# Down products of an FFN in pairs from block 0 on with a last group of four, and raw weights in twelve places of 2 KB

## The chip, the cores and the metric

The kernel runs on one core of a Trainium2 chip. The metric is the device time of one execution in microseconds, here the median of three runs. The engines are named as the profile names them: PE (TensorE matmul), PEld (its weight load), DVE (VectorE), ACT (ScalarE), POOL (GpSimd) and SP (SyncE, which issues every DMA of this kernel).

## What is computed

The input is 512 tokens `x` and 256 context tokens `ctx` of width 1024. The first block has two layers. Each layer is a half FFN, a mixer and a second half FFN, and each of them has its own norm, shift, scale and gate, all from one conditioning product (`ada_w`). In the last layer's second half the context is no longer needed. The second block is a gated delta rule branch and a dilated window attention branch. Cut to what matters here:

```
def swiglu(x, w_gu, w_down):
    gt, up = jnp.split(x @ w_gu, 2, axis=-1)
    return (jax.nn.silu(gt) * up) @ w_down

def half_ffn(h, g, shift, scale, gate, w_gu, w_down):
    return h + 0.5 * gate * swiglu(norm_mod(h, g, shift, scale), w_gu, w_down)

def first_block(...):
    for li in range(2):
        m = jnp.split((silu(c) @ ada_w[li] + ada_b[li]), 9)       # and mc from c_ctx
        h = half_ffn(h, norm_g[li, 0], m[0], m[1], m[2], ffn_w_gu[li, 0], ffn_w_down[li, 0])
        z = norm_mod(h, norm_g[li, 1], m[3], m[4])
        h = h + m[5] * mixer(z, zc)
        h = half_ffn(h, norm_g[li, 2], m[6], m[7], m[8], ffn_w_gu[li, 1], ffn_w_down[li, 1])
        # the same for the context hc, up to the second layer's mixer
```

`w_gu` is 1024 x 5632 and `w_down` 2816 x 1024, all in float32. There are four FFNs.

## The kernel before

**Number format.** Every float32 operand of a large product is split into a high part (`hi`, rounded for PE by an ACT copy) and the rest (`lo`, a DVE subtraction): `split`, `halves`. A product is then three matmuls, hi·hi, hi·lo, lo·hi (`mm3`).

**Raw weights.** `raw` (line 737) loads a piece of a weight matrix by a DMA on SP into a place of the tag `raw`. There are `RAW` = 5 places of 128 x 1024 float32, 4 KB on each partition, 512 KB in all. `split` makes `whi` and `wlo` of it, 512 columns at a time, in `PARTS` = 10 places each. A place is free again once the last reader of all of its 4 KB is done. The gates (`load_gate`, line 866), rows of 1024 values broadcast to all partitions, take places of the same tag, and hold them as long as they are needed.

**The FFN** (`ffn`, line 1071). The 2816 hidden features are 22 blocks of 128. For each block `gate_up` (line 1017) loads the two 1024 x 128 weight blocks and makes seven combinations of their quarters, `swiglu` runs seven products on half of the tokens each (banks named `gu`), and writes the activations `ah` and `al`, three places each. The down products (`down(g)`, line 1083) run over groups of blocks: for each tile of 128 tokens and each half of 512 columns, the blocks of the group are summed in one PSUM bank (`dn`), and the bank is then taken into the running sum `h`. The first group's bank is copied by ACT, that of later groups added by DVE, that of the last but one is added, multiplied by the gate and added to the residual `hin`, and that of the last is multiplied by the gate and added, after which the tile goes to `on_tile`: its norm, its transposes and what the next stage needs of it. Line 1078 sets the groups:

```
groups = [[0]] + [[f, f + 1] for f in range(1, NF - 4, 2)] + [list(range(NF - 3, NF))]
```

These are block 0 alone, nine pairs, and blocks 19 to 21. A group's down products are issued one block late, after `swiglu` of the block that follows the group's last one. In the loop over blocks `filler(f)` puts in conditioning units: `ada` (line 817) runs one 1024 x 512 part of `ada_w` in two halves of four matmuls that work side by side, and later fills the `mods` and gates.

The first three FFNs run on six tiles (768 tokens, `gu` matmuls of 384 columns), the last on four (256 columns). The stages are: FFN 1 (to about 595 us), the even mixer with its output product (to about 905 us), FFN 2 (to about 1460 us), FFN 3 (to about 1995 us), the odd mixer (to about 2265 us), FFN 4 (to about 2640 us), the second block.

**What sets the order.** The code above doesn't issue instructions; it records them (`Engine`, `Program.record`). `Program.order` (line 505) then plays a list scheduler with a cost for each instruction, counts the places of each tag, takes for each engine the earliest recorded instruction that can start, may move some between DVE, ACT and POOL (`others`), and `emit` writes the result in that order (line 693, which is why all instructions have that line). Each engine runs its list in order. So a change in places or groups moves instructions elsewhere too. An FFN's phase has `SCR` = 8 scratch places of 2 KB.

Of the kernel before, what the change touches and what calls it, by code (L numbers as in the profile page):

```python
# [10 lines left out]
F32 = mybir.dt.float32  # L11
F32R = mybir.dt.float32r
# [8 lines left out]
D = 1024  # L21
# [298 lines left out]
        ("gpsimd", "gpsimd"): 0.1}  # L320

KEEP = 1
RAW, PARTS = 5, 10
SCR = 8
CPLAN = "1567234"
XN = "vv"
PARK = "vavavava"
# [372 lines left out]
class Net:  # L700
# [34 lines left out]
        return self.t2(name).rearrange("p (a b) -> p a b", a=4)  # L735

    def raw(self, src, a, b):
        v = self.wp.tile([128, 1024], F32, tag="raw", name="raw", bufs=RAW)[:, :a * b].rearrange("p (a b) -> p a b", a=a)
        self.nc.sync.dma_start(v, src)
        return v  # L740

# [28 lines left out]

    def w_cols(self, w, c0, ncol, nk=KD, pool=None):
        ws = []
        kk = 1024 // ncol
        for k0 in range(0, nk, kk):
            ws += self.split(self.raw(w[k0 * 128:(k0 + kk) * 128, c0:c0 + ncol].rearrange("(k p) c -> p k c", p=128),
                                      kk, ncol), pool=pool if k0 < 4 else None)
        return ws

    def w_feats(self, w, c0):
        ws = [], []  # L780
        for k0 in (0, 512):
            r = self.raw(w[k0:k0 + 512, c0:c0 + 256].rearrange("(k p) c -> p k c", p=128), 4, 256)
            for i in range(2):
                ws[i].extend(self.split(r[:, :, i * 128:(i + 1) * 128]))
        return ws

    def proj_t(self, cols, ws):
# [29 lines left out]
    def ada(self, li, n):  # L817
        self.ada_end()


        nc, T = self.nc, self.T
        S = self.bank("ada")
        for k0 in (0, 4):
            r = [self.raw(T["ada_w"][li][k * 128:(k + 2) * 128, n * 512:(n + 1) * 512]
                          .rearrange("(k p) c -> p k c", p=128), 2, 512) for k in (k0, k0 + 2)]
            with nc.together(4):
                for k in range(k0, k0 + 4):
                    c = 32 * (k % 4)
                    nc.tensor.matmul(S[c:c + 32, :], self.scp[:, k, :], r[k % 4 // 2][:, k % 2, :],
                                     start=(k < 4), stop=(k >= 4), tile_position=(0, c))  # L830
        Ss = self.t2("adaSs")
        nc.vector.tensor_copy(Ss, S)
        self.open_ada.append((li, n, Ss))
# [32 lines left out]
    def load_gate(self, li, gi, nx=2):  # L866
        g = []
        for x in range(nx):
            t = self.wp.tile([128, D], F32, tag="raw", name=f"gate{x}", bufs=RAW)
            self.nc.sync.dma_start(t, self.gated[li, gi][x:x + 1, :].to_broadcast([128, D]))  # L870
            g.append(t)
        return g

    def rstd(self, ss, n, scale, eps):
# [142 lines left out]
    def gate_up(self, li, which, f):  # L1017

        nc = self.nc
        src = self.T["ffn_gu"][2 * li + which][f]  # L1020
        r = [self.raw(src[:, k:k + 4, :], 4, 256) for k in (0, 4)]
        a11, a12 = (x[:, :, 0:128] for x in r)
        a21, a22 = (x[:, :, 128:256] for x in r)
        s1, s2 = self.t24("ws"), self.t24("ws")
        sub = lambda d, x, y: nc.vector.tensor_tensor(d, x, y, op=OP.subtract)
        ws = {1: self.split(a11)}
        nc.gpsimd.tensor_tensor(s1, a21, a22, op=OP.add)
        sub(s2, s1, a11)
        ws[6] = self.split(s2)
        ws[5] = self.split(s1)  # L1030
        sub(a21, a11, a21)
        ws[7] = self.split(a21)
        ws[2] = self.split(a12)
        sub(a12, a12, s2)
        ws[3] = self.split(a12)
        ws[4] = self.split(a22)
        return ws
# [33 lines left out]
    def ffn(self, li, which, nt, F, hsrc, filler, on_tile, first=None):  # L1071
# [3 lines left out]
        ntok = nt * 128  # L1075
        n = ntok // 2
        z = self.operands(F.zx, n)
        groups = [[0]] + [[f, f + 1] for f in range(1, NF - 4, 2)] + [list(range(NF - 3, NF))]
        ends = [g[-1] for g in groups]
        acts = {}  # L1080
        gates = []
# [1 line left out]
        def down(g):  # L1083
            ws = {}
            for f in g:
                r = self.raw(wd[f * 128:(f + 1) * 128, :].rearrange("p (a b) -> p a b", a=2), 2, 512)
                ws[f] = self.split(r)
            left = len(groups) - 1 - groups.index(g)
            if left == 1:
                gates.extend(self.load_gate(li, 2 * which, 2 if nt > 4 else 1))  # L1090
            for t in range(nt):
                cs = at(t, nt)
                for half in range(2):
                    hs = slice(half * 512, (half + 1) * 512)
                    if left == 1:
                        x = self.t2("hin")
                        nc.sync.dma_start(x, hsrc(t)[:, hs])
                    ps = self.bank("dn")
                    self.mm3(ps, [(tuple(a[:, cs] for a in acts[f]), ws[f][half]) for f in g])
                    y = F.h[t][:, hs]  # L1100
                    if left == 0:
                        if HADD[t + 6 - nt] == "g":
                            tmp = self.t2("dtmp")
                            nc.vector.tensor_mul(tmp, ps, gates[0 if t < 4 else 1][:, hs])
                            nc.gpsimd.tensor_add(y, y, tmp)
                        else:
                            nc.vector.tensor_mul(ps, ps, gates[0 if t < 4 else 1][:, hs])
                            nc.vector.tensor_add(y, y, ps)
                    elif g[0] == 0:
                        nc.scalar.copy(y, ps)  # L1110
                    else:
                        nc.vector.tensor_add(y, y, ps)
                    if left == 1:
                        nc.vector.tensor_mul(y, y, gates[0 if t < 4 else 1][:, hs])
                        nc.gpsimd.tensor_add(y, y, x)
                if left == 0:
                    on_tile(t)

        F.new_h(nt)
        for f in range(NF):  # L1120
            ws = first if first and f == 0 else self.gate_up(li, which, f)
            acts[f] = tuple(F.ap.tile([128, ntok], F32R, tag=x, name=x, bufs=3) for x in ("ah", "al"))
            self.swiglu(ws, z, n, *acts[f], *([ORD0, "15"] if first and f == 0 else []))
            self.late = []
            filler(f)
# [6 lines left out]
    def out_proj(self, w, tiles0, hsrc, h, gates, on_tile):  # L1132
# [4 lines left out]
        for half, tiles in ((0, tiles0), (1, range(len(h)))):  # L1137
            hs = slice(half * 512, (half + 1) * 512)
            ws = self.w_cols(w, half * 512, 512)
            for t in tiles:  # L1140
                ps = self.proj_t(at(t, len(h)), ws)
                tmp = self.t2("otmp")
                nc.vector.tensor_mul(tmp, ps, gates[0 if t < 4 else 1][:, hs])
                (nc.vector if OADD[half] == "v" else nc.gpsimd).tensor_add(h[t][:, hs], h[t][:, hs], tmp)
                if half == 1:
                    on_tile(t)
# [408 lines left out]
    def dn_head(self, h, M, C, Pm, st, ones):  # L1555
# [16 lines left out]

        ws = []
        for c in (h, 4 + h, 8 + h, 12 + h):
            ws.append(self.split(self.raw(w_in[:, c * 128:(c + 1) * 128].rearrange("(k p) c -> p k c", p=128), KD, 128)))
        feats = []
        for i in range(4):
            ps = self.bank("dnp")
# [490 lines left out]
def layout(inputs):  # L2069
    a = {k: np.asarray(v) for k, v in inputs.items()}  # L2070
    arrays = {n: np.ascontiguousarray(a[n]) for n in _INS}
    arrays["ffn_gu"] = np.ascontiguousarray(
        a["ffn_w_gu"].reshape(4, KD, 128, 2, NF, 128).transpose(0, 4, 2, 1, 3, 5)).reshape(4, NF, 128, KD, 256)
    w = a["ev_w_out"][0]
    arrays["ev_w_out"] = np.concatenate([w[:512].reshape(2, 4, 64, D).transpose(1, 0, 2, 3).reshape(512, D), w[512:]])
    rpb = np.pad(a["d_rpb"][0], ((0, 0), (0, 0), (16, 16)))
# [24 lines left out]
```

## Time and profile before

| | |
|---|---|
| median of three runs | 3287.4 us (3286.73 to 3289.97) |
| profiled execution, device time | 3290.94 us |
| its span | 3289.0 us |
| PE busy | 3205.9 us (97%), 18198 matmul records |
| DVE busy | 2348.6 us (71%) |
| ACT busy | 1347.3 us (41%) |
| POOL busy | 263.2 us (8%) |
| DMA | 337.70 MB, mean 103 GB/s |
| mean granted clock of PE | 0.991 |

The span is the time from the first to the last profiled instruction; the device time of the same execution has 1.94 us around it. A float32 matmul that isn't split (`ada`, the transposes aside) shows as two records. Busy time of PE counts time under a lower granted clock as busy, so a loss can sit in the clock column of a stretch that looks full.

### The profile page before, as it was taken

How to read it: one execution, taken by the hardware profiler on the slowest of the kernel's cores; microseconds unless marked ns; L12 is line 12 of the kernel's file. 1: busy time of each engine (PE TensorE's matmuls, PEld its weight loads, DVE VectorE, ACT ScalarE, POOL GpSimd, SP SyncE). 2: the span in 40 equal slices, each digit the busy share in tenths (PEclk: the TensorE clock that was granted, in tenths of full speed). 3: DMA queues.
4: the chain of work that ended last, by engine and by line, in shares of the span. 5: the costliest groups of instructions: out<-in, count | busy, mean ns of one | idle time of the engine just before them, and what ended most of it. 6: DMA issues, size and time to landing. Idle time of an engine off the chain costs nothing.

```text
span 3289.0 us, 47391 instructions
## 1 busy us (share of the span) xinstructions
PE 3205.9 (97%) x18198; PEld 2796.0 (85%) x18198; DVE 2348.6 (71%) x4531; ACT 1347.3 (41%) x2773; POOL 263.2 (8%) x276
## 2 busy tenths in 40 slices
PE   7999999999999999989999999999999999999999
PEld 4889998776778999969999988867999888898987
DVE  7677768777677767797767786677888977667343
ACT  5333333644453333354333335445444444444331
POOL 0000001212100000010000002110000112231000
PEclk9999999999999999999999999999999999999999
DMA  7342123222444221252221233253322341121221
GB/s 258 119 158 78 65 70 122 94 78 90 154 163 148 77 74 62 91 188 85 77 77 58 72 121 102 83 176 124 113 99 97 123 144 46 39 77 61 90 90 64
DMA packets 161522, 337.70 MB, mean 103 GB/s; under 512 B 12256, under 2 KB 57696, under 8 KB 161168
## 3 DMA queue, kind: packets, MB, share of 16 engines
q1 hardware_dynamic: 161296, 334.68, 30.6%
q8 instruction: 143, 2.34, 0.3%
q14 instruction: 83, 0.68, 0.1%
HBM read 316.76 MB, written 17.87 MB: 102 GB/s over the span
## 4 chain that ended last, share of the span: by engine, by line
PE 86%; DVE 9%; DMA 2%; ACT 2%; issue 1%; POOL 0%; SPq 0%; ACTq 0%; DVEq 0%; POOLq 0%
PE gu L693 34%; PE dn L693 18%; PE pj L693 14%; PE pjf L693 5%; DVE h L693 2%; PE dnp L693 2%; PE ada L693 2%; PE sc L693 1%; PE tr L693 1%; PE fin L693 1%; PE yb L693 1%; PE dmm L693 1%; PE pv L693 1%; PE ptr L693 1%; DMA raw<-in_ffn_gu 1%
## 5 line engine op out<-in xcount | busy, mean ns | idle before, releaser
L693 ACT CAST whi<-raw 128x512 fp32r<-128x512 f32 x885 | 522.7, 620 | 665.7 <-PE gu L693 198.5
L693 DVE TENSOR_TENSOR wlo<-raw,whi 128x512 fp32r<-128x512 f32 (+1 forms) x846 | 560.7, 688 | 233.6 <-ACT whi L693 216.8
L693 DVE TENSOR_TENSOR gu<-gu 128x384 f32<-128x384 f32 (+1 forms) x616 | 319.5, 519 | 273.8 <-PE gu L693 260.8
L693 DVE TENSOR_TENSOR h<-h,dn 128x512 f32<-128x512 f32 x404 | 273.3, 681 | 67.3 <-PE dn L693 67.0
L693 PE MATMUL dn<-wlo,ah 128*128 128x512 f32 x968 | 310.9, 395 | 0.0
L693 PE MATMUL dn<-whi,ah 128*128 128x512 f32 x968 | 307.5, 396 | 0.0
L693 PE MATMUL dn<-whi,al 128*128 128x512 f32 x968 | 305.6, 395 | 0.0
L693 PE MATMUL gu<-zh,whi 128*128 128x384 f32 (+1 forms) x1408 | 287.9, 326 | 13.2 <-ACT zh L693 4.6
L693 PE MATMUL gu<-zh,wlo 128*128 128x384 f32 (+1 forms) x1408 | 288.5, 323 | 0.0
L693 PE MATMUL gu<-zl,whi 128*128 128x384 f32 (+1 forms) x1408 | 283.3, 322 | 0.2 <-DVE zl L693 0.2
L693 PEld LDWEIGHTS gu<-zh,whi 128*128 128x128 f32 x1408 | 237.4, 189 | 33.8 <-ACT zh L693 8.4
L693 PEld LDWEIGHTS gu<-zl,whi 128*128 128x128 f32 x1408 | 235.6, 189 | 3.8 <-DVE zl L693 2.4
L693 PEld LDWEIGHTS gu<-zh,wlo 128*128 128x128 f32 x1408 | 237.4, 190 | 0.0
L693 PE MATMUL gu<-zxh,wlo 128*128 128x384 f32 (+1 forms) x1056 | 219.1, 326 | 8.1 <-DVE wlo L693 8.1
L693 PE MATMUL gu<-zxh,whi 128*128 128x384 f32 (+1 forms) x1056 | 214.5, 328 | 1.9 <-ACT zxh L693 1.0
L693 PEld LDWEIGHTS dn<-wlo,ah 128*128 128x128 f32 x968 | 182.1, 188 | 40.0
L693 ACT CAST whi<-ws 128x512 fp32r<-128x512 f32 x176 | 105.8, 620 | 268.6 <-PE dn L693 212.6
L693 PEld LDWEIGHTS dn<-whi,al 128*128 128x128 f32 x968 | 181.8, 188 | 38.5 <-DVE al L693 0.2
L693 PE MATMUL gu<-zxl,whi 128*128 128x384 f32 (+1 forms) x1056 | 214.2, 325 | 0.0
L693 PEld LDWEIGHTS dn<-whi,ah 128*128 128x128 f32 x968 | 180.0, 189 | 37.5 <-ACT ah L693 1.9
L693 PE MATMUL pj<-whi,zh 128*128 128x512 f32 (+1 forms) x848 | 199.2, 369 | 6.1 <-ACT swP L693 3.1
L693 PEld LDWEIGHTS gu<-zxh,whi 128*128 128x128 f32 x1056 | 180.0, 190 | 21.3 <-issue 3.4
(391 smaller groups left out, 5225.8 us busy)
## 6 DMA issues: line engine op xcount, KB each, us to landing
raw<-in_ffn_gu SPq DMA_DIRECT2D x176, 512.0 KB
raw<-in_ada_w SPq DMA_DIRECT2D x144, 512.0 KB
raw<-in_ffn_w_down SPq DMA_DIRECT2D x88, 512.0 KB
raw<-in_w_in SPq DMA_DIRECT2D x72, 512.0 KB
raw<-in_od_w_in SPq DMA_DIRECT2D x16, 512.0 KB
raw<-in_ev_w_in SPq DMA_DIRECT2D x14, 512.0 KB
gate<-gate SPq DMA_DIRECT2D x10, 512.0 KB
raw<-in_ev_w_out SPq DMA_DIRECT2D x8, 512.0 KB
```

The costliest lines, as they stand in the source:

```text
L693: getattr(self.real[o.eng], o.fn)(*[real(x) for x in o.args], **{k: real(v) for k, v in o.kw.items()})
```

## The change

The first group is blocks 0 and 1, followed by eight more pairs, and the last group is blocks 18 to 21; the last but one group's gate and residual work so follows block 18 instead of 19. Activations have four places instead of three. A raw place is 2 KB and there are twelve: every load is at most 512 float32 on each partition, and the host lays `ffn_gu` out so that each quarter of a block's weights is one contiguous load. A gate is two loads. An FFN's phase has nine scratch places, and the program's scratch for dynamic DMAs is set to 1024 bytes.

```
-RAW, PARTS = 5, 10
-SCR = 8
+RAW, PARTS = 12, 10
+SCR = 9
...
     def raw(self, src, a, b):
-        v = self.wp.tile([128, 1024], F32, tag="raw", name="raw", bufs=RAW)[:, :a * b].rearrange("p (a b) -> p a b", a=a)
+        v = self.wp.tile([128, 512], F32, tag="raw", name="raw", bufs=RAW)[:, :a * b].rearrange("p (a b) -> p a b", a=a)
...
     def w_cols(self, w, c0, ncol, nk=KD, pool=None):
-        kk = 1024 // ncol
+        kk = 512 // ncol
...
     def w_feats(self, w, c0):
-            r = self.raw(w[k0:k0 + 512, c0:c0 + 256].rearrange("(k p) c -> p k c", p=128), 4, 256)
             for i in range(2):
-                ws[i].extend(self.split(r[:, :, i * 128:(i + 1) * 128]))
+                c = c0 + 128 * i
+                ws[i].extend(self.split(self.raw(w[k0:k0 + 512, c:c + 128].rearrange("(k p) c -> p k c", p=128), 4, 128)))
...
     def ada(self, li, n):
-            r = [self.raw(T["ada_w"][li][k * 128:(k + 2) * 128, n * 512:(n + 1) * 512]
-                          .rearrange("(k p) c -> p k c", p=128), 2, 512) for k in (k0, k0 + 2)]
+            r = [self.raw(T["ada_w"][li][k * 128:(k + 1) * 128, n * 512:(n + 1) * 512].unsqueeze(1), 1, 512)
+                 for k in range(k0, k0 + 4)]
...
     def load_gate(self, li, gi, nx=2):
-            t = self.wp.tile([128, D], F32, tag="raw", name=f"gate{x}", bufs=RAW)
-            self.nc.sync.dma_start(t, self.gated[li, gi][x:x + 1, :].to_broadcast([128, D]))
-            g.append(t)
+            g.append([self.wp.tile([128, 512], F32, tag="raw", name=f"gate{x}", bufs=RAW) for _ in range(2)])
+            for i, t in enumerate(g[x]):
+                self.nc.sync.dma_start(t, self.gated[li, gi][x:x + 1, i * 512:(i + 1) * 512].to_broadcast([128, 512]))
...
     def gate_up(self, li, which, f):
-        r = [self.raw(src[:, k:k + 4, :], 4, 256) for k in (0, 4)]
-        a11, a12 = (x[:, :, 0:128] for x in r)
-        a21, a22 = (x[:, :, 128:256] for x in r)
+        a11, a21, a12, a22 = (self.raw(src[:, i], 4, 128) for i in range(4))
...
     def ffn(self, li, which, nt, F, hsrc, filler, on_tile, first=None):
-        groups = [[0]] + [[f, f + 1] for f in range(1, NF - 4, 2)] + [list(range(NF - 3, NF))]
+        groups = [[f, f + 1] for f in range(0, NF - 4, 2)] + [list(range(NF - 4, NF))]
...
-                r = self.raw(wd[f * 128:(f + 1) * 128, :].rearrange("p (a b) -> p a b", a=2), 2, 512)
-                ws[f] = self.split(r)
+                ws[f] = [self.split(self.raw(wd[f * 128:(f + 1) * 128, c:c + 512].unsqueeze(1), 1, 512))[0]
+                         for c in (0, 512)]
...
-            acts[f] = tuple(F.ap.tile([128, ntok], F32R, tag=x, name=x, bufs=3) for x in ("ah", "al"))
+            acts[f] = tuple(F.ap.tile([128, ntok], F32R, tag=x, name=x, bufs=4) for x in ("ah", "al"))
...
     def dn_head(self, h, M, C, Pm, st, ones):
-            ws.append(self.split(self.raw(w_in[:, c * 128:(c + 1) * 128].rearrange("(k p) c -> p k c", p=128), KD, 128)))
+            ws.append([w for k in (0, 512) for w in self.split(self.raw(
+                w_in[k:k + 512, c * 128:(c + 1) * 128].rearrange("(k p) c -> p k c", p=128), 4, 128))])
...
-    nc = bacc.Bacc("TRN2", target_bir_lowering=False, num_devices=1)
+    nc = bacc.Bacc("TRN2", target_bir_lowering=False, num_devices=1, dynamic_dma_scratch_size=1024)
```

In the order that the scheduler writes, PE keeps its 18198 records' worth of matmuls; DVE's adds of `dn` into `h` go from 404 to 360, and SP's DMAs from 723 to 1275. Three places on PE show what moves. In the names, `gu` are the seven products of a block, `dn` the down products, `ada` one half of a conditioning unit for each x4, `tr` the transposes of a normed tile `xn`, and `adaSs` a conditioning result. A row is a run of like matmuls.

First, blocks 0 and 1 of FFN 1, before:

```order
L693 MATMUL gu<-zh,wlo 128x384 x4
L693 MATMUL gu<-zl,whi 128x384 x4
L693 MATMUL adag<-adaSs,constA 2x512
L693 MATMUL dn<-whi,ah 128x512 x3
L693 MATMUL gu<-zh,whi 128x384 x4
L693 MATMUL gu<-zxh,whi 128x384 x4
L693 MATMUL gu<-zh,wlo 128x384 x4
L693 MATMUL gu<-zl,whi 128x384
```

and now:

```order
L693 MATMUL gu<-zh,wlo 128x384 x4
L693 MATMUL gu<-zl,whi 128x384 x4
L693 MATMUL gu<-zxh,whi 128x384 x4
L693 MATMUL gu<-zxh,wlo 128x384 x4
L693 MATMUL gu<-zxl,whi 128x384 x4
L693 MATMUL adag<-adaSs,constA 2x512
L693 MATMUL gu<-zxh,whi 128x384 x4
L693 MATMUL gu<-zh,whi 128x384 x2
```

The down products of block 0 no longer stand between the products of blocks 0 and 1; the first `dn` row now stands some 35 rows further on, in block 2.

Second, the hand-over from the even mixer's output product to FFN 2, before:

```order
L693 MATMUL tr<-constA,xn 128x128 x20
L693 MATMUL ada<-raw,scp 32x512 x4
L693 MATMUL tr<-constA,xn 128x128 x10
L693 MATMUL ada<-raw,scp 32x512 x4
L693 MATMUL tr<-constA,xn 128x128 x2
L693 MATMUL gu<-zh,whi 128x384 x4
```

and now:

```order
L693 MATMUL tr<-constA,xn 128x128 x20
L693 MATMUL ada<-raw,scp 32x512 x8
L693 MATMUL tr<-constA,xn 128x128 x12
L693 MATMUL tr<-constA,adaSs 128x128 x4
L693 MATMUL ada<-raw,scp 32x512 x8
L693 MATMUL gu<-zh,whi 128x384 x4
```

Four halves of conditioning units stand ahead of the first `gu` matmul where two stood.

Third, the hand-over from FFN 2 to FFN 3, from the last down matmuls on, before:

```order
L693 MATMUL dn<-whi,al 128x512
L693 MATMUL ada<-raw,scp 32x512 x4
L693 MATMUL tr<-constA,xn 128x128 x8
L693 MATMUL ada<-raw,scp 32x512 x4
L693 MATMUL tr<-constA,xn 128x128 x16
L693 MATMUL ada<-raw,scp 32x512 x8
L693 MATMUL gu<-zh,whi 128x384 x4
```

and now:

```order
L693 MATMUL dn<-whi,al 128x512 x4
L693 MATMUL ada<-raw,scp 32x512 x4
L693 MATMUL tr<-constA,xn 128x128 x4
L693 MATMUL ada<-raw,scp 32x512 x4
L693 MATMUL tr<-constA,xn 128x128 x4
L693 MATMUL ada<-raw,scp 32x512 x4
L693 MATMUL tr<-constA,xn 128x128 x8
L693 MATMUL tr<-constA,adaSs 128x128 x4
L693 MATMUL ada<-raw,scp 32x512 x8
L693 MATMUL gu<-zh,whi 128x384 x4
```

After the last down matmul 16 transposes of `xn` are left where 24 were, and five halves of conditioning units stand ahead of the first `gu` matmul where four stood.

## Rows read from the trace of the kernel before

**Rows 1.** The page's first part: engine, busy us (share of the span), instructions.

```profile
PE 3205.9 (97%) x18198; PEld 2796.0 (85%) x18198; DVE 2348.6 (71%) x4531; ACT 1347.3 (41%) x2773; POOL 263.2 (8%) x276
```

**Rows 2.** Stretches of 50 us: length, busy us (instructions) per engine, clock, DMA share.

```profile
core 0: us, PE busy (x) PEld busy (x) DVE busy (x) ACT busy (x) POOL busy (x), PEclk, DMA share, GB/s
500.00:550.00 50.00, 47.75 (x246) 43.63 (x246) 44.49 (x72) 15.02 (x27) 7.45 (x5) 1.00 0.33 106
...
1150.00:1200.00 50.00, 50.00 (x259) 46.09 (x258) 36.29 (x63) 15.55 (x28) 0.00 (x0) 1.00 0.18 64
...
2550.00:2600.00 50.00, 44.77 (x315) 42.19 (x314) 46.26 (x83) 20.36 (x40) 4.29 (x3) 0.93 0.32 106
```

**Rows 3.** Stretches of 10 us around block 1 and the hand-overs, same columns.

```profile
70.00:80.00 10.00, 10.00 (x57) 9.67 (x56) 9.22 (x17) 5.31 (x11) 2.90 (x1) 1.00 0.41 129
80.00:90.00 10.00, 10.00 (x51) 8.90 (x50) 7.91 (x14) 7.38 (x15) 0.36 (x1) 1.00 0.25 84
...
900.00:910.00 10.00, 6.96 (x44) 4.58 (x42) 8.41 (x16) 7.77 (x17) 2.57 (x3) 0.95 0.62 189
910.00:920.00 10.00, 8.74 (x34) 4.43 (x35) 9.60 (x18) 6.66 (x13) 0.00 (x0) 0.54 0.52 184
...
1450.00:1460.00 10.00, 5.84 (x33) 2.22 (x31) 8.85 (x17) 6.78 (x18) 5.16 (x5) 1.00 0.61 209
1460.00:1470.00 10.00, 7.93 (x36) 3.94 (x37) 8.31 (x17) 7.69 (x15) 1.26 (x1) 0.66 0.95 318
1470.00:1480.00 10.00, 9.30 (x49) 6.05 (x49) 9.17 (x16) 3.50 (x7) 0.00 (x0) 1.00 0.99 359
...
2300.00:2310.00 10.00, 8.59 (x62) 7.73 (x62) 7.83 (x15) 4.27 (x9) 0.00 (x0) 1.00 0.43 130
```

**Rows 4.** PE in order of time: start us, us, instructions, [idle before <-releaser].

```profile
43.48 1.05 PE L693 MATMUL ada<-raw,scp 128*32 128x512 f32 x4 [1.71 <-DMA raw<-in_ada_w]
...
905.44 1.07 PE L693 MATMUL ada<-raw,scp 128*32 128x512 f32 x8 [0.41 <-ACT h L693]
...
2588.12 0.80 PE L693 MATMUL gu<-zxh,wlo 128*128 128x256 f32 x2 [5.19 <-DVE wlo L693]
```

**Rows 5.** The page's costliest groups: busy us, mean ns | idle before, releaser.

```profile
L693 DVE TENSOR_TENSOR wlo<-raw,whi 128x512 fp32r<-128x512 f32 (+1 forms) x846 | 560.7, 688 | 233.6 <-ACT whi L693 216.8
L693 DVE TENSOR_TENSOR h<-h,dn 128x512 f32<-128x512 f32 x404 | 273.3, 681 | 67.3 <-PE dn L693 67.0
```

**Rows 6.** PE in order of time, two down matmuls in a row.

```profile
88.11 0.40 PE L693 MATMUL dn<-wlo,ah 128*128 128x512 f32 x1
88.34 0.40 PE L693 MATMUL dn<-whi,al 128*128 128x512 f32 x1
```

**Rows 7.** SP in order of time around the hand-over to FFN 3.

```profile
1417.77 0.38 SPq L693 DMA_DIRECT2D raw<-in_ada_w  x1
...
1442.90 0.38 SPq L693 DMA_DIRECT2D raw<-in_ada_w  x1
...
1457.90 0.81 SPq L693 DMA_DIRECT2D hC<-h  x2
```

**Rows 8.** Waits of SP's queue: us in total, times, longest us.

```profile
SPq L693 <- DVE wlo L693: 1991.4, 343, 50.9
```

**Rows 9.** Stretches of 5 us at the start, columns as in rows 2.

```profile
20.00:25.00 5.00, 3.90 (x30) 1.74 (x28) 1.87 (x8) 3.38 (x7) 0.55 (x1) 1.00 1.04 391
25.00:30.00 5.00, 2.76 (x12) 0.74 (x12) 4.79 (x11) 4.35 (x8) 0.00 (x0) 1.00 0.89 305
30.00:35.00 5.00, 3.76 (x17) 2.48 (x17) 5.00 (x10) 2.75 (x6) 0.00 (x0) 0.68 0.58 197
35.00:40.00 5.00, 5.00 (x35) 3.28 (x27) 4.96 (x10) 2.40 (x5) 0.00 (x0) 0.98 0.64 207
40.00:45.00 5.00, 2.58 (x12) 0.29 (x8) 0.85 (x4) 0.00 (x0) 0.00 (x0) 1.00 0.78 268
```

**Rows 10.** Waits of PE's weight load: us in total, times, longest us.

```profile
PEld ada L693 <- issue: 23.5, 82, 1.8
```

More of the change, by code (lines that the diff above doesn't have):

```diff
@@ L828, in ada @@
                     c = 32 * (k % 4)
-                    nc.tensor.matmul(S[c:c + 32, :], self.scp[:, k, :], r[k % 4 // 2][:, k % 2, :],
+                    nc.tensor.matmul(S[c:c + 32, :], self.scp[:, k, :], r[k % 4][:, 0, :],
                                      start=(k < 4), stop=(k >= 4), tile_position=(0, c))
@@ L1103, in down @@
                             tmp = self.t2("dtmp")
-                            nc.vector.tensor_mul(tmp, ps, gates[0 if t < 4 else 1][:, hs])
+                            nc.vector.tensor_mul(tmp, ps, gates[0 if t < 4 else 1][half])
                             nc.gpsimd.tensor_add(y, y, tmp)
                         else:
-                            nc.vector.tensor_mul(ps, ps, gates[0 if t < 4 else 1][:, hs])
+                            nc.vector.tensor_mul(ps, ps, gates[0 if t < 4 else 1][half])
                             nc.vector.tensor_add(y, y, ps)
@@ L1113, in down @@
                     if left == 1:
-                        nc.vector.tensor_mul(y, y, gates[0 if t < 4 else 1][:, hs])
+                        nc.vector.tensor_mul(y, y, gates[0 if t < 4 else 1][half])
                         nc.gpsimd.tensor_add(y, y, x)
@@ L1142, in out_proj @@
                 tmp = self.t2("otmp")
-                nc.vector.tensor_mul(tmp, ps, gates[0 if t < 4 else 1][:, hs])
+                nc.vector.tensor_mul(tmp, ps, gates[0 if t < 4 else 1][half])
                 (nc.vector if OADD[half] == "v" else nc.gpsimd).tensor_add(h[t][:, hs], h[t][:, hs], tmp)
@@ L2072, in layout @@
     arrays["ffn_gu"] = np.ascontiguousarray(
-        a["ffn_w_gu"].reshape(4, KD, 128, 2, NF, 128).transpose(0, 4, 2, 1, 3, 5)).reshape(4, NF, 128, KD, 256)
+        a["ffn_w_gu"].reshape(4, 2, 4, 128, 2, NF, 128).transpose(0, 5, 3, 1, 4, 2, 6)).reshape(4, NF, 128, 4, 4, 128)
     w = a["ev_w_out"][0]
```

## The prediction

> **What bounds the kernel now.** I read the page's first part, then the span cut into stretches of 50 us, then stretches of 10 us where PE was short of full, and last the waits inside those.
>
> PE is busy 3205.9 us of 3289.0; 83.1 us are idle, and DVE, the next engine, is at 71% [rows 1]. The reader is to see that the idle time is not spread out. In the steady middle of an FFN (1150 to 1200 us) PE shows 50.00 of 50 at clock 1.00 while DVE has 13.7 us free; nothing that frees another engine can pay there [rows 2]. The loss sits where one stage hands over to the next. From 900 to 920 us (mixer to second FFN) PE idles 3.04 + 1.26 us and the granted clock falls to 0.54; from 1450 to 1480 us (second to third FFN) it idles 4.16 + 2.07 + 0.70 us and the clock falls to 0.66; near the end of the last FFN (2550 to 2600 us) 5.23 us and 0.93 [rows 2, 3]. [...] The idle gaps themselves name a raw `ada_w` load (43.48 us), the norm chain (905.44, after ACT wrote `h`), and a DVE split (2588.12, 5.19 us) [rows 4]. So what decides is how much other PE work, with its weights already on the chip, lies ready at the hand-overs.
>
> **The change, part by part.**
>
> *Groups.* Each FFN has ten down groups instead of eleven. PE's matmuls are the same in number and shape. What goes is one PSUM eviction per half tile and FFN, 12 + 12 + 12 + 8 = 44, at 681 ns on DVE: 30.0 us [rows 5]. In the middle of the FFNs PE covers all of it: 0 us. Without that cover it would be worth up to the 30 us.
>
> *The last group.* A group of four blocks runs 12 matmuls per half tile where three ran 9. At 0.23 us from start to start [rows 6] that is 2.76 instead of 2.07 us, so the last group of a six-tile FFN lasts 33.1 instead of 24.8 us. The norm of tile t runs under the matmuls of the tiles behind it, and has 8.3 us more to do so. The order shows it at the hand-over from second to third FFN: 16 transposes of `xn` are left after the last `dn` matmul, 24 before. With it goes the use of the raw places. At 1417.77 us SP could issue one `ada_w` load and the next only at 1442.90 [rows 7]: two of five places held gates and two the next block's weights. Now gates hold 4 of 12 and a block's weights 4, which leaves 4 small places, a whole half of an `ada` unit. The stretch loses 6.93 us idle and 3.4 us of clock, 10.3 in all. I take half, -5; bounds -10.3 and +1.7 (one more wait for a load, as at 43.48 [rows 4]).
>
> At the mixer's hand-over the new order puts four halves of `ada` ahead of the first `gu` matmul, two before. A half takes 1.07 us [rows 4], so 2.1 us of work from later, full stretches fill idle time; with a little of the clock I take -3; bounds -9.4 (4.3 idle, 5.1 clock [rows 3]) and +1.7. Ends of the first and third FFN: PE idles 2.25 us from 500 to 550 us [rows 2], and about as much in the third. That is the burst of the last pair (add, gate, residual: 12 x 3 x 0.68 = 24.5 us of DVE), which only moves one block earlier; behind it on DVE wait the next block's splits, and PE for these. The longer last group takes a little of the norm's wait: -1; bounds -4.5 and +1.7. Last FFN: same burst, 8 x 3 x 0.68 = 16.3 us, same 5.19 us gap, a block earlier: 0; bounds -8.7 (5.2 idle, 3.5 clock) and +5.2, the gap a second time. The gate and `hin` loads move with the burst, ahead of one more block's weights on SP; 16 issues at 0.4 us [rows 7] are 6.4 us in a queue that mostly waits.
>
> *The first group.* Block 0's down products no longer come with block 1 but with block 2. That takes 36 matmuls, 8.3 us, from a place where DVE is nearly full (9.22 and 7.91 of 10 us from 70 to 90 us [rows 3]); they come back a block later. DVE gains its 2.9 free us and two splits less (2 x 0.69 [rows 5]), so at most 8.3 - 2.9 - 1.4 = 4.0 us are exposed in each six-tile FFN; in the four-tile one 24 x 0.23 - 1.4 - 2.2 free from 2300 to 2310 us [rows 3] = 1.9. Bounds 0 and +13.9. I take +3, since only the first and the last FFN have DVE that full.
>
> *Twelve places of 2 KB.* SP issues 1275 DMAs instead of 723. At 0.4 us the 552 more take 221 us [rows 7], beside 1991 us that SP spends waiting for DVE to free a place [rows 8]: 0 us. At the start the reader is to see loads that wait for places: the DMA share falls from 1.04 (20 to 25 us) to 0.89, 0.58, 0.64, 0.78 [rows 9], 1.27 x 5 = 6.4 us of transfer time missing while PE waits for `ada_w` at 43.48 us. Room for three halves of `ada` in place of two and a half should win back half: -3; bounds -6.4 and +1.7. Each half now waits for four loads where it waited for two: 144 more waits on PE. The nearest row is 23.5 us in 82 stops of the weight load before `ada` [rows 10], 0.29 us each, so between 0 and +41 us; PE's matmuls run on through those stops, so I take 0.
>
> [...] Bytes moved well at the large size: 391 GB/s from 20 to 25 us in pieces of 512 KB, with several in flight [rows 9]. [...]
>
> *The fourth place for activations, the ninth scratch place and the small DMA scratch* change no order in the full stretches and no DMA is issued off SP: 0.
>
> **Sum.** -5 - 3 - 1 + 0 + 3 + 0 - 3 + 0 = -9 us. On the profiled execution's own 3290.94 that is 3281.9; that execution lies 3.5 us over the median of the runs, 3287.4, so for the median: 3278.4 us.
>
> **Rivals.** (a) No change: the hand-overs are bound by the norm chain alone, and work put into one hole is missing in the next. For it: the gap at 905.44 waits for ACT's `h`, not for a load. Against it: SP's gap from 1417.77 to 1442.90. Time: 3287. (b) Slower: the first group's missing filler. If DVE is as full at block 1 of every FFN as at 70 to 80 us, the 13.9 us come and the hand-overs return nothing: 3301. It decides once DVE shows over 9.5 of 10 us at block 1 with PE idle on `wlo` or `gu`. Against it: the chain at the start begins earlier too, and the mixed order of `gu` products. (c) More: the holes close far enough for the clock to stay up. Half of 6.4 + 9.4 + 10.3 + 4.5 + 8.7 = 39.3 gives -20: 3268. (d) Half-size pieces move at half the rate. The five stretches from 20 to 45 us hold 19.7 us of transfers that PE waits for [rows 9]; twice that is 3287 + 20 = 3307. The share of 0.18 from 1150 to 1200 us would double and still hide [rows 2]. [...]
>
> **How the numbers follow.** Forecast 0.50 (0.42 of it beyond 0.2%), (a) 0.20, (b) 0.15, (c) 0.13, (d) 0.02. About 0.2%, 6.6 us, is what a measurement can tell from no change. Faster: 0.42 + 0.13 = 0.55. Same: 0.08 + 0.20 + 0.02 of (b) = 0.30. Slower: 0.13 + 0.02 = 0.15. The forecast's own range is 3270 to 3285; the range reaches to 3264 for (c) and to 3296 for most of (b).
>
> **What would show it.** Right: PE idle and clock at the two hand-overs better by some 3 and 5 us, DMA share over 0.8 from 25 to 45 us and no `ada_w` wait of over 1 us there, DVE 30 us less busy, PE's full stretches the same. Wrong: idle of PE on `wlo` at block 1 or 2 of an FFN, PE stops before `ada`, or a DMA share near 1 in the middle of an FFN.

## The result and the profile after

The changed kernel takes 3254.46 us (median of 4 runs, 3252.87 to 3260.82) against 3288.68 us before: ratio 0.9898, 95% interval 0.988 to 0.9915. That is 34 us faster where 9 were forecast: 15.5 us below the forecast's own range, which began at 3270, and 9.5 below the 3264 to which rival (c) stretched it. The profiled execution took 3252.87 us with a span of 3251.1 us at clock 0.996, which is 37.9 us less than the span before. A second set of 5 runs of the same kernel, in another session, gave 3257.75 us (0.9897, 0.9883 to 0.9912).

The page's first part, which answers to [rows 1]:

```profile
PE 3188.3 (98%) x18198; PEld 2789.9 (86%) x18198; DVE 2315.7 (71%) x4486; ACT 1352.5 (42%) x2778; POOL 263.4 (8%) x272
```

PE is busy 17.6 us less with as many matmuls, which fits the mean clock of 0.996 for 0.991 (0.005 of 3251 is 16 us); the other 20.3 us were idle time. DVE is 32.9 us less busy; the evictions were counted at 30.0. The groups of [rows 5] now:

```profile
L693 DVE TENSOR_TENSOR wlo<-raw,whi 128x512 fp32r<-128x512 f32 x855 | 566.7, 687 | 255.7 <-ACT whi L693 240.1
L693 DVE TENSOR_TENSOR h<-h,dn 128x512 f32<-128x512 f32 x360 | 243.6, 681 | 71.8 <-PE dn L693 71.5
```

Stretches of 10 us (columns as in [rows 2]) around block 1, then the hand-over from the mixer to FFN 2, then that from FFN 2 to FFN 3, which answer to [rows 3]:

```profile
70.00:80.00 10.00, 10.00 (x59) 10.00 (x58) 8.84 (x16) 2.04 (x4) 0.00 (x0) 1.00 0.34 102
80.00:90.00 10.00, 10.00 (x56) 7.80 (x55) 8.38 (x16) 5.84 (x12) 0.00 (x0) 1.00 0.60 177
...
880.00:890.00 10.00, 7.86 (x60) 4.29 (x59) 9.46 (x19) 9.91 (x22) 0.86 (x1) 1.00 0.73 242
890.00:900.00 10.00, 9.81 (x38) 4.41 (x38) 9.75 (x17) 8.76 (x17) 0.00 (x0) 1.00 1.01 358
...
1420.00:1430.00 10.00, 6.31 (x36) 3.12 (x35) 9.83 (x22) 7.97 (x19) 1.72 (x2) 1.00 0.73 242
1430.00:1440.00 10.00, 9.16 (x47) 3.88 (x48) 9.54 (x17) 7.71 (x16) 0.00 (x0) 1.00 1.00 353
```

The reader is to see the clock column: 1.00 in both hand-overs, where 0.54 and 0.66 stood. The first has 2.33 us idle instead of 4.30, the second 4.53 instead of 6.93. At the second, waits for `ada_w` loads fell from 2.2 to 0.4 us; what is left waits for the norm (`xn`, 3.6 us). The start, against [rows 9] and one row more:

```profile
20.00:25.00 5.00, 4.21 (x33) 2.03 (x32) 1.64 (x7) 2.74 (x8) 0.55 (x1) 1.00 1.05 387
25.00:30.00 5.00, 3.52 (x13) 1.11 (x14) 4.76 (x11) 4.52 (x9) 0.00 (x0) 1.00 1.05 387
30.00:35.00 5.00, 5.00 (x24) 2.62 (x21) 4.90 (x9) 3.38 (x7) 0.00 (x0) 1.00 1.03 361
35.00:40.00 5.00, 4.94 (x32) 2.70 (x30) 4.97 (x9) 2.24 (x4) 0.00 (x0) 1.00 0.72 242
40.00:45.00 5.00, 3.68 (x15) 1.06 (x16) 4.64 (x14) 3.65 (x7) 0.00 (x0) 1.00 0.88 293
45.00:50.00 5.00, 5.00 (x23) 3.22 (x22) 5.00 (x9) 5.00 (x10) 0.00 (x0) 1.00 1.02 362
```

The row that follows on [rows 9], before:

```profile
45.00:50.00 5.00, 4.67 (x20) 1.32 (x20) 3.72 (x10) 3.16 (x6) 0.00 (x0) 0.66 1.05 386
```

From 30 to 50 us PE's idle time fell from 3.99 to 1.38 us, and the clock, 0.68, 0.98, 1.00 and 0.66 before and 1.00 throughout after, gave back 3.4 us: 6.0 us in all.

The longest wait of PE for an `ada_w` load after the first is 0.72 us; 1.71 stood in [rows 4]. The last row there, the burst of FFN 4, is now:

```profile
2532.82 0.74 PE L693 MATMUL gu<-zxh,wlo 128*128 128x256 f32 x4 [3.82 <-DVE wlo L693]
```

None of this reaches 34 us. What the prediction never cut finer is FFN 1 behind the start. In stretches of 50 us, before:

```profile
50.00:100.00 50.00, 48.22 (x256) 41.76 (x253) 39.69 (x70) 28.46 (x54) 3.26 (x1) 1.00 0.41 136
100.00:150.00 50.00, 49.04 (x263) 41.35 (x262) 34.75 (x61) 15.31 (x28) 0.00 (x0) 1.00 0.46 153
150.00:200.00 50.00, 48.97 (x266) 41.90 (x265) 33.57 (x61) 14.69 (x27) 0.00 (x0) 1.00 0.43 148
```

and after:

```profile
50.00:100.00 50.00, 49.89 (x268) 41.44 (x267) 44.26 (x79) 24.09 (x45) 3.94 (x1) 1.00 0.58 190
100.00:150.00 50.00, 49.81 (x275) 43.33 (x274) 24.94 (x47) 21.92 (x40) 0.00 (x0) 1.00 0.36 114
150.00:200.00 50.00, 50.00 (x275) 43.26 (x274) 31.50 (x58) 14.28 (x26) 0.00 (x0) 1.00 0.46 154
```

Before, PE is short of full by 1.78, 0.96 and 1.03 us; after, by 0.30 in all three together. FFN 1 gains 7.3 us up to block 4 (the moved down products, 36 x 0.232 = 8.35 us, counted back), 2.1 from there to block 18 and 2.2 behind it. So most of it lies towards the start: over the whole FFN idle time gives 7.0 us (10.35 before, 3.39 after) and the clock 3.4, all of that ahead of block 4.

To compare many kernels, each trace is cut at PE's own marks: an FFN runs from the start of its first `gu` to that of its last `dn` matmul, a mixer from there to the next FFN's first `gu` (so it has the output product and one hand-over in it). Before, the six stretches last 558.1, 326.0, 536.6, 524.6, 274.4 and 356.9 us. The table gives each kernel's median, its ratio to before in the same session, and by how many us its profiled execution's stretches differ from those. "Room" is places times size in KB. Outside the six stretches lie the start, the hand-over from FFN 2 to FFN 3 and the second block, +2.3 us in the new kernel's first row.

| kernel | room, groups | us | ratio (95%) | FFN 1 | even mixer | FFN 2 | FFN 3 | odd mixer | FFN 4 |
|---|---|---|---|---|---|---|---|---|---|
| new | 12x2 new | 3254.46 | 0.9898 (0.9880-0.9915) | -11.6 | -11.7 | -7.6 | -4.0 | -2.5 | -2.8 |
| new_again | 12x2 new | 3257.75 | 0.9897 (0.9883-0.9912) | -12.0 | -8.1 | -7.1 | -3.7 | -4.4 | 0.0 |
| places_only | 12x2 old | 3278.12 | 0.9963 (0.9951-0.9976) | -14.2 | -1.2 | -3.8 | -6.0 | +7.7 | +0.8 |
| groups_only | 5x4 new | 3297.93 | 1.0024 (1.0015-1.0033) | +9.6 | -9.4 | +2.7 | +8.2 | -1.9 | -3.3 |
| fine_same_room | 10x2 new | 3279.48 | 0.9968 (0.9956-0.9980) | +2.8 | -11.0 | -2.0 | +3.6 | -2.5 | -3.1 |
| eleven_places | 11x2 new | 3267.09 | 0.9929 (0.9916-0.9941) | -2.2 | -14.0 | +0.3 | -4.9 | -1.6 | -3.7 |
| thirteen_places | 13x2 new | 3255.26 | 0.9895 (0.9881-0.9909) | -12.1 | -9.3 | -8.0 | -3.9 | -4.2 | -1.1 |
| coarse_more_room | 6x4 new | 3263.28 | 0.9918 (0.9905-0.9932) | -11.7 | -2.0 | -2.6 | +0.6 | -2.8 | -4.1 |
| old_groups_more_room | 6x4 old | 3270.07 | 0.9936 (0.9922-0.9949) | -13.1 | -7.7 | +2.8 | -5.9 | +1.1 | -0.8 |
| last_of_four | 12x2 mixed | 3281.29 | 0.9972 (0.9960-0.9984) | -2.4 | -9.8 | -3.4 | +5.1 | -1.5 | -4.0 |
| first_pair | 12x2 mixed | 3299.24 | 1.0027 (1.0017-1.0036) | -5.4 | -0.1 | -0.7 | +5.1 | +8.2 | +2.0 |

The two rows of the new kernel show the scatter between executions: 0.5 us in the FFNs 1 to 3, up to 4 in the mixers and FFN 4, where the clock differs between the two (1.00 in new and 0.97 in new_again from 650 to 700 us, 0.93 and 0.86 from 2200 to 2250, 0.97 and 0.93 from 2500 to 2550).

### The profile page after: what moved, and what is told of

Its sections match the earlier page's. It is cut to its first block, busy times and chain, and to the rows that moved or that the text cites. A ratio compares the mean times of both kernels' runs of the same rounds, so it can differ in the third digit from the quotient of the medians.

```text
span 3251.1 us, 48859 instructions
## 1 busy us (share of the span) xinstructions
PE 3188.3 (98%) x18198; PEld 2789.9 (86%) x18198; DVE 2315.7 (71%) x4486; ACT 1352.5 (42%) x2778; POOL 263.4 (8%) x272
## 4 chain that ended last, share of the span: by engine, by line
PE 85%; DVE 9%; DMA 2%; ACT 2%; issue 1%; SPq 0%; POOL 0%; DVEq 0%; ACTq 0%
PE gu L693 34%; PE dn L693 17%; PE pj L693 13%; PE pjf L693 5%; DVE h L693 3%; PE dnp L693 2%; PE ada L693 2%; PE fin L693 1%; PE sc L693 1%; PE yb L693 1%; PE dmm L693 1%; PE tr L693 1%; PE pv L693 1%; DVE wlo L693 1%; PE ptr L693 1%
## 5 line engine op out<-in xcount | busy, mean ns | idle before, releaser
L693 DVE TENSOR_TENSOR wlo<-raw,whi 128x512 fp32r<-128x512 f32 x855 | 566.7, 687 | 255.7 <-ACT whi L693 240.1
L693 PE MATMUL dn<-whi,ah 128*128 128x512 f32 x968 | 300.1, 396 | 0.0
L693 PE MATMUL dn<-wlo,ah 128*128 128x512 f32 x968 | 298.5, 395 | 0.0
L693 DVE TENSOR_TENSOR h<-h,dn 128x512 f32<-128x512 f32 x360 | 243.6, 681 | 71.8 <-PE dn L693 71.5
L693 PEld LDWEIGHTS dn<-whi,al 128*128 128x128 f32 x968 | 180.9, 188 | 37.9
```

Source lines behind the costliest of these rows:

```text
L693: getattr(self.real[o.eng], o.fn)(*[real(x) for x in o.args], **{k: real(v) for k, v in o.kw.items()})
```

## Experiments

**The parts alone.** Two theories stood against each other, that the places (T1) or that the groups (T2) carry the gain, and a third, that it is luck of the scheduler's order (T3).

places_only, the new kernel with:

```
-SCR = 9
+SCR = 8
-        groups = [[f, f + 1] for f in range(0, NF - 4, 2)] + [list(range(NF - 4, NF))]
+        groups = [[0]] + [[f, f + 1] for f in range(1, NF - 4, 2)] + [list(range(NF - 3, NF))]
-            ... name=x, bufs=4) for x in ("ah", "al"))
+            ... name=x, bufs=3) for x in ("ah", "al"))
```

> The new kernel with the old groups (block 0 alone, last group of three), three places for activations and eight scratch places; the twelve raw places of 2 KB and the half-size loads stay. T1 (the places carry the gain, by weights that lie ready at the start, in the mixer and at the hand-overs): 3262 us, some 26 of the 34 us; the even mixer (FFN 1's last dn to FFN 2's first gu) 11 us shorter than before's 326. T2 (the groups carry it, by the longer last group and 30 us less of DVE): 3279 us, hand-overs as before. T3 (the list scheduler's other order is luck, above all in the mixer): total between 3255 and 3285, mixer anywhere from 314 to 326.

groups_only, the kernel before with the reverse of these lines and the DMA scratch (so in both runs the fourth activation place and the ninth scratch place go with the groups; the activation place was never run by itself):

> The kernel before with the new groups, four places for activations, nine scratch places and the small DMA scratch; five raw places of 4 KB as before. T1: 3281 us (-6, the longer last group at the two hand-overs), the mixer as before within 2 us, the start as before. T2: 3262 us (-26), DVE 30 us less busy and the FFNs' ends 5 us each shorter. T3: 3260 to 3285, mixer anywhere from 314 to 326.

fine_same_room, the new kernel with `RAW` 10:

> The new kernel with ten raw places of 2 KB, the same 20 KB as before. T1 in the form that the finer grain counts (a place comes free after half as much work): within 6 us of the new kernel, 3254 to 3260. T1 in the form that the room counts (24 KB for 20): half of the gain or more is gone, 3270 or more. T2: 3254 to 3258. T3: 3250 to 3275.

coarse_more_room, the kernel before with the new groups, four activation places, `SCR` 9, `RAW` 6 and the DMA scratch:

> The kernel before with the new groups, four places for activations, nine scratch places and six raw places of 4 KB (the 24 KB of the new kernel in the old pieces). T1 with grain: 3278 us, within 5 us of the kernel with the new groups alone. T1 with room: 3260. T2: 3260. T3: 3255 to 3285.

Measured 3278.12, 3297.93, 3279.48 and 3263.28 us. Neither T1 nor T2 holds: each part alone brings a third of the gain or a loss. T3's range for the total, 3255 to 3285, fails for groups_only. In FFN 1 the room sorts the kernels: FFN 1 gains 11.6 to 14.2 us in every one of these kernels with 24 KB, whatever its groups and pieces (the two mixed kernels, below, lose it again at the end), and is longer than before in both new ones with 20 KB. The totals need room and groups together. With 20 KB in the old pieces the new groups cost 8 us; with 24 KB in the old pieces the kernel gains 27; and places_only, with 24 KB and the old groups, is level with fine_same_room, with 20 KB and the new ones. Ten small places in place of twelve lose 25 us, and the table says where: FFN 1 14.4, FFN 2 5.6, FFN 3 7.6, the mixers and FFN 4 under 1 each. Inside FFN 1 that is 5.4 us up to block 4, 5.8 to block 18 and 3.2 behind it; of the 14.4, PE's idle time shows 8.2 and its clock 1.7.

What is short shows in SP's rows for every second one of the first nine blocks of FFN 1 (start us, us from the first issue of the row to the end of its last). Before, block 5:

```profile
143.82 16.46 SPq L693 DMA_DIRECT2D raw<-in_ffn_gu  x2
```

In groups_only block 4 with its neighbours, and where PE stands in it:

```profile
119.07 16.66 SPq L693 DMA_DIRECT2D raw<-in_ffn_gu  x2
135.82 8.20 SPq L693 DMA_DIRECT2D raw<-in_ada_w  x4
147.72 4.67 SPq L693 DMA_DIRECT2D raw<-in_ffn_w_down  x2
152.48 0.86 SPq L693 DMA_DIRECT2D raw<-in_ffn_gu  x2
```

```profile
140.47 0.97 PE L693 MATMUL gu<-zh,whi 128*128 128x384 f32 x4 [1.53 <-ACT whi L693]
```

The first half of the block's weights is issued at 119.07 us and the second only 16 us later, when a place comes free. It is out at 135.7 us, 0.4 us before the block's first product (136.15); the splits come late and PE stands 1.53 us at the second product. Before it was the same: out at 160.3, first product at 160.70, 0.96 us of wait. In the new kernel, block 6:

```profile
150.56 13.90 SPq L693 DMA_DIRECT2D raw<-in_ffn_gu  x4
```

The four quarters are still spread over 13.9 us, but the last is out at 164.5 us, 16.6 us before the block's first product (181.08): a whole block earlier, and PE does not stand there. The blocks between go out together in all three, in 0.9 us (152.48 above) to 3.4 us.

**Room alone, how much of it, and the mixer's order.** old_groups_more_room is the kernel before with `RAW` 6 and the DMA scratch; thirteen_places and eleven_places change `RAW` of the new kernel.

> The kernel before with six raw places of 4 KB instead of five and nothing else but the small DMA scratch that makes the room; old groups. Room theory (24 KB let a block's second load start before the conditioning units' loads): FFN 1 some 12 us shorter as with twelve small places (-14), the mixer as before, in all 3276 us, within 4 of the kernel with twelve small places and old groups (3278). Rival (the room pays only with the new groups, which need more of it): 3286 to 3290.

> The new kernel with thirteen raw places of 2 KB instead of twelve; the mixer's order on PE is the same. Room theory: the FFNs' blocks no longer wait for loads with twelve, so little is left: 3251 to 3256 us. Rival (each 2 KB pay as the last two did, 25 us for the step from ten to twelve): 3242 us.

> The new kernel with eleven raw places of 2 KB; the even mixer's order on PE is the same. Set theory (a block's four pieces, one conditioning half's four and a pair's four down pieces are twelve, and one less makes the block's last piece wait behind a conditioning half): FFN 1 slower than the new kernel by 7 us or more, the whole 3265 us or more. Smooth theory (half of the 25 us from ten to twelve): 3267 us, with FFN 1, 2 and 3 each at the middle. Rival (a threshold at eleven): 3254 to 3258.

Measured 3270.07, 3255.26 and 3267.09 us. One more 4 KB place, and nothing else but the DMA scratch, brings 18 us to the kernel before; its FFN 1 is 13.1 us shorter and full, and its block 5 has its last piece out at 137.4 us, 16.6 us before its first product:

```profile
100.00:150.00 50.00, 50.00 (x269) 42.61 (x268) 33.21 (x59) 14.91 (x27) 1.39 (x1) 1.00 0.46 153
150.00:200.00 50.00, 50.00 (x276) 43.44 (x275) 33.51 (x61) 16.19 (x30) 0.00 (x0) 1.00 0.43 148
```

```profile
129.03 8.34 SPq L693 DMA_DIRECT2D raw<-in_ffn_gu  x2
```

Its even mixer, expected as before, was 7.7 us shorter as well, so not all of the 18 us is the FFNs'. More places also give the scheduler another order inside the FFNs, and the two were not taken apart there; the late piece is the link that the rows show.

With 10, 11, 12 and 13 small places the new kernel takes 3279, 3267, 3254 to 3258 and 3255 us: room pays up to twelve and not beyond. Twelve is what one block, one half of `ada` and one pair's down weights take, four pieces each. By its total eleven places fit the set theory and the smooth one. Block 4 of FFN 1 speaks for the set: with eleven its last piece is out at 131.7 us, 0.5 us before its first product (132.19), as with ten, and PE stands 0.94 us:

```profile
101.60 30.14 SPq L693 DMA_DIRECT2D raw<-in_ffn_gu  x4
```

FFN 3 fits neither theory: with eleven it gains 4.9 us, no less than with twelve.

Of the even mixer's 11.7 us the room explains nothing: it is long (coarse_more_room) and short (groups_only) with either. PE's order in it differs between kernels, since the scheduler's list forks (what is left of T3). So two kernels were run with each other's order: the 1022 matmuls of the even mixer may leave PE's list only in a given sequence.

```
+        pe = [o for o in self.ops if o.eng == "tensor"]
+        line = [pe[2860 + int(i)] for i in MIXER.split()]
+        nth = {o: i for i, o in enumerate(line)}
+        done = 0
...
                 for rk, o, x in avail[e][:600]:
+                    if nth.get(o, done) != done:
+                        continue
...
             out.append(o)
+            done += o in nth
```

> The kernel with six raw places of 4 KB and the new groups (3263.28 us), but the even mixer's 1022 matmuls on PE are held to the order in which the new kernel issues them; nothing else is prescribed. Fork (the 11 us of the mixer are a fork in the list scheduler's order, whatever the places): from FFN 1's last down matmul to the first mix matmul 200 us instead of 211, the whole 3253 us. Rival (the small places themselves make the mixer shorter: its weights come earlier): 211 us and 3263 us as before the swap.

> The new kernel (3254.46 us) with the even mixer's matmuls on PE held to the order of the kernel with six places of 4 KB. Fork: 211 us for the mixer's part instead of 199.7, the whole 3265 us. Rival (the small places): 200 us and 3254 us.

From FFN 1's last down matmul to the first `mix` matmul it was 201.4 us (211.4 with its own order) and 212.3 (199.7). The totals: 3258.08 us, 0.9904 (0.9889 to 0.992), which its interval doesn't separate from 0.9918 unswapped; and 3269.07 us, 0.9938 (0.9925 to 0.9952), 13 us slower than the new kernel and separated from it. So the order's worth shows in the total one way only. Stretches of 30 us in the new kernel:

```profile
640.00:670.00 30.00, 29.44 (x215) 22.08 (x213) 21.56 (x65) 12.09 (x38) 3.43 (x4) 1.00 0.04 12
670.00:700.00 30.00, 28.40 (x208) 19.49 (x207) 23.93 (x72) 16.26 (x50) 4.16 (x3) 1.00 0.60 183
700.00:730.00 30.00, 29.58 (x212) 23.07 (x212) 23.11 (x62) 16.11 (x45) 3.90 (x4) 1.00 0.17 54
```

and in new_mixer_swapped:

```profile
640.00:670.00 30.00, 24.12 (x154) 18.69 (x152) 19.34 (x58) 11.54 (x38) 2.94 (x3) 0.89 0.00 1
670.00:700.00 30.00, 29.38 (x219) 22.37 (x218) 20.45 (x63) 13.37 (x39) 2.72 (x3) 1.00 0.00 1
700.00:730.00 30.00, 27.02 (x203) 17.46 (x200) 22.83 (x69) 14.26 (x44) 2.91 (x2) 1.00 0.37 107
```

The worse order leaves PE idle 5.9 and 3.0 us of 30 in two of the three stretches, and the clock falls to 0.89 with the first.

**Does the order alone do it in kernels with the old groups?** The same lines, with groups_only's order in the kernel before, and with the new kernel's order of both mixers in places_only and old_groups_more_room.

> The kernel before, unchanged but for the order of the even mixer's 1022 matmuls on PE, which is held to the order in the kernel with the new groups and the old places (199.7 us there, 211.0 before). Fork: 200 to 202 us, the whole 3278 us, 10 less than before, with nothing of the change in it. Rival (the shorter mixer needs the new groups' entry: the longer last group leaves the norms further on): 207 us or more, the whole 3285 us or more.

> The kernel with twelve small places and the old groups (3278.12 us), with both mixers' matmuls on PE held to the new kernel's order. Fork: the even mixer 10 us shorter and the odd one 10 us shorter (282.1 to 272), the whole 3258 us; what is left to the new kernel's 3254.5 is what the groups themselves are worth, 3 to 4 us. Rival (the groups carry most of their 24 us, and the mixers are a part of that): 3268 us or more.

> The kernel before with six places of 4 KB (3270.07 us), with both mixers' matmuls on PE held to the new kernel's order. Fork and room: even mixer 205.7 to 200 us, odd mixer 275.5 to 272, the whole 3261 us: 27 of the 34 us with the old groups and the old pieces, by room and order alone. Rival (small pieces and new groups are needed for more than 10 us): 3268 us or more.

Measured 3288.71 us (0.9993, 0.9984 to 1.0002), 3277.99 and 3270.42: no gain in any that stands clear of the noise. The even mixer's stretch up to `mix` went to 203.7, 205.8 and 203.9 us from 211.0, 210.1 and 205.7, so the good order gives less behind the old groups than the 199.7 to 202.5 behind the new ones. The odd mixer got no shorter (+9.4 where +7.7 stood, +5.5 where +1.1 stood). My fork theory falls for the odd mixer, and for the even one it is part of the story; that the rest is what the FFN's end leaves to do is argued, not shown.

**The beginning or the end of the groups.** The new kernel with one half of the old groups each:

```
last_of_four
+        groups = [[0]] + [[f, f + 1] for f in range(1, NF - 6, 2)] + [[NF - 5], list(range(NF - 4, NF))]
first_pair
+        groups = [[f, f + 1] for f in range(0, NF - 4, 2)] + [[NF - 4], list(range(NF - 3, NF))]
```

> The new kernel with the old beginning of the groups (block 0 alone, then pairs) and the new end (block 17 alone, then 18 to 21), eleven groups as before; all else new. Entry theory (the longer last group covers the norms at the end of FFN 1, 2 and 3, and so sets how the mixers start and which order the scheduler gives them): both mixers within 2 us of the new kernel's, FFN 1's first blocks some 2 us shorter, since block 0's down products fill again; the whole 3252 to 3260 us, at least 18 of the 24 us between old and new groups. Rival (one group and 44 evictions less is what pays): 3272 us or more.

> The new kernel with the new beginning of the groups (pairs from block 0 on) and the old end (block 18 alone, then 19 to 21), eleven groups; all else new. Entry theory: the even mixer 10 us and the odd one 5 to 10 us longer than in the new kernel, the whole 3272 to 3282 us, like the old groups with twelve small places (3278). Rival (the first pair pays): 3262 us or less.

In these two the mixers follow the end of the groups, as the entry theory said: -9.8 and -1.5 us with the last group of four, -0.1 and +8.2 without. For the even mixer that is not the whole of it: it was hardly shorter in coarse_more_room, with the new end (-2.0), and shorter in old_groups_more_room, with the old one (-7.7). The totals are 3281.29 and 3299.24 us. The first misses the entry theory and lies where its rival (one group and 44 evictions less is what pays) put it, the second misses both. But in both kernels the two parts of FFN 1 up to block 18 are within 0.4 us of the new kernel's, with the moved work counted in, so block 0 as a group of its own costs nothing there; the loss lies behind it, 9.1 and 6.4 us. Both have a single block as last group but one. Its burst of add, gate and residual then has half as many matmuls to lie under, and PE stands in FFN 1 (the same shows in FFN 3). PE of last_of_four in order of time:

```profile
515.73 1.65 PE L693 MATMUL gu<-zxh,wlo 128*128 128x384 f32 x4 [6.16 <-DVE wlo L693]
```

The entry is seen at the odd mixer, in order of time on PE, in places_only:

```profile
1972.64 0.86 PE L693 MATMUL dn<-whi,al 128*128 128x512 f32 x3
1977.61 1.97 PE L693 MATMUL tr<-constA,xn 128*128 128x128 f32 x8 [4.11 <-ACT xn L693]
1982.23 0.58 PE L693 MATMUL pj<-whi,zh 128*128 128x256 f32 x1 [2.65 <-ACT zh L693]
```

and in the new kernel:

```profile
1958.25 1.09 PE L693 MATMUL dn<-whi,al 128*128 128x512 f32 x4
1959.18 0.63 PE L693 MATMUL pj<-whi,zh 128*128 128x256 f32 x4
```

The first `pj` product follows the last down matmul at once in every kernel with a last group of four; before it came 2.0 us after that matmul's start, in places_only and first_pair 9.1.

**The scratch places.** `SCR` 8 and 10 in the new kernel, and the new kernel beside the latter:

> The new kernel with eight scratch places instead of nine. Forecast of the prediction (nothing): 3252 to 3258 us. Rival (the ninth place lets the end of an FFN, with residual loads and products in scratch, run ahead): 3260 us or more, lost at the ends of the FFNs.

> The new kernel with ten scratch places instead of nine. Scratch theory (from eight to nine they brought 5 us, in FFN 1 and at the hand-over behind FFN 2; the next brings part of it): 3248 to 3252 us, faster than the new kernel run beside it. Rival (nine suffice, and the 5 us of eight places are scatter of the order): 3253 to 3259 us, the same as the new kernel beside it.

> The new kernel unchanged, beside the kernel with ten scratch places, so that the two are compared on one chip in one session: 3252 to 3259 us, its mixers 199 to 202 us and 271 to 274 us as before.

Measured 3259.44 us (0.9906, 0.9892 to 0.9919), 3251.12 (0.9886, 0.9871 to 0.9901) and 3257.75. The intervals overlap. With eight places FFN 1 gains 8.9 us instead of 11.6 and 12.0, so the ninth may carry 3 us; with ten the FFNs 1 to 3 are within 0.8 us of the new kernel's. Ten places gave the lowest median of all, but it isn't shown to beat the new kernel.

## Why the prediction was wrong

**The step that failed is the term "Twelve places of 2 KB", -3 us.** It priced the room only where loads are seen to wait at the start, and bounded the gain there at 6.4. One more 4 KB place brings 18 us to the kernel before, and going from ten to twelve small places is worth 25 us of medians in the new one, nearly all inside the FFNs. The start itself, from 30 to 50 us, gave 6.0 us, inside that bound, though more than half of it is clock, which the term did not have. What it missed are the rounds behind the start. I had read the middle of the FFNs from one stretch, 1150 to 1200 us, which is full [rows 2], and said that nothing which frees another engine pays there. But FFN 1 was short of full by 1.0 to 1.8 us in each 50 from 50 to 200 us. PE's named waits there come to 3.5 us, 1.8 of them for `whi` and 0.4 for an `ada_w` load; after, neither is left. SP's long waits for a place, which I used as cover for more issues [rows 8], were themselves the delay: in FFN 1, up to block 8, they held the last piece of every second block back until the block began.

fine_same_room is the change without the room: 3279.48 us, 11 us less than before, near the 9 I summed. That is luck: its even mixer, which the sum did not have, is 11.0 us shorter, and its FFN 1 and 3 are 2.8 and 3.6 us longer.

**The even mixer was missing from the sum.** 11.7 us in one profiled execution and 8.1 in the other. The swaps show one cause, PE's order there, worth 10 to 13 us of that stretch behind the new groups. A second, the entry behind the longer last group, is argued from the two half changes and not separated from the order. Why the scheduler's list forks where it does isn't settled.

**The hand-overs: right in mechanism, sized low.** FFN 2 to FFN 3 was put at -5: idle time and clock give 2.4 + 3.4 = 5.8 us. The mixer's at -3: 2.0 idle + 5.1 clock = 7.1, inside its bound of 9.4; I had taken a little of the clock, and it stayed up whole. In new_again the clock dips there again (0.97 over 50 us in each), and the same count gives 3.6 and 4.9 us, so some of this comes and goes. These stretches reach into the table's FFN 2 and FFN 3; the two counts do not add. The clock's part in these sums is my estimate: what the column lacks of 1.00, times the length of the stretch. In the trace before, the column reads 0.50 in every us from 910 to 919, and four `gu` matmuls there take 1.42 us from start to start (916.76 to 918.18) where four of the same shape in FFN 1, at 1.00, take 0.69 (54.53 to 55.22).

**The ends of FFN 1 and 3, -1.** From block 18 to the last `dn` they are 2.2 and 2.4 us shorter, with the moved 8.3 us of down products counted back. The term gave this to the longer last group, and that is the wrong way round: with the room and the old groups (places_only) they are 4.7 and 5.0 us shorter, so the new groups cost some 2.5 us there, and what they bring comes behind it, in the mixers.

**The first group, +3.** Measured nothing: block 4 starts 5.7 us earlier than before in last_of_four, which keeps block 0 alone, and 5.8 in the new kernel with the moved work counted back, and PE is full from 70 to 90 us. Rival (b)'s time came near with 20 KB, where groups_only took 3297.93 us, but not by its mechanism: of the 9.6 us that FFN 1 is longer there, 7.8 lie between block 4 and block 18, and 0.6 ahead of it. The new groups need the room.

**At nothing, and rightly:** SP's issues, the waits ahead of `ada` (weight load behind issue 27.2 us in 82 stops, 6.7 of them the first load of all; [rows 10] had 23.5), the last FFN's burst (3.82 us for 5.19, FFN 4 -2.8 and 0.0). Rival (d) fell: pieces of 256 KB moved 387 GB/s from 20 to 30 us. Rival (c), the clock staying up, was the nearest at 3268, and still 13.5 us short.

## What to carry to other kernels

Count the room that one round of the steady loop needs in loads (here a block, a filler half and a pair of down blocks, twelve pieces) before a regrouping. In this kernel, with fewer, the last piece of every second block in the first half of FFN 1 went out as the block began; a thirteenth place bought nothing. Cut every stage into its own stretches: "full in the middle", read from one stretch of FFN 2, hid a part of what FFN 1 had to give, and what ten places would have cost the new groups. Where a list scheduler writes the order, a change of pools can move a far stage by 10 us, and two kernels with their orders swapped help to tell this from an effect of the resource.

## What the runs showed that I had not expected

The clock stayed at 1.00 in this execution through a stretch with 3.69 us idle of 10 (1420 to 1430 us), where 0.66 followed 4.16 idle before; in another execution of the same kernel it read 0.97 over the 50 us there. The same program's span was 3251.1 and 3258.3 us in two profiled executions, with mean clocks of 0.996 and 0.993, and nearly all of the difference lies in the mixers, their hand-overs and FFN 4.
